# A decoder trunk on one Trainium2 core: side engines issued in source order through the Strassen groups of the feed-forward layers, with their first loads three steps sooner

## The chip, the cores and the metric

One core of one Trainium2 chip runs the whole program. The metric is the device time of one execution in microseconds (us). The profiled execution gives, beside its own time, a span: the time from its first to its last recorded instruction. TensorE (PE in the profile) does the matmuls, VectorE (DVE) and ScalarE (ACT) the elementwise work, GpSimd (POOL) a little arithmetic and the accumulating DMAs, and sync (SP) starts the plain weight loads.

## The reference

Two layers, float32, a sequence of 512 tokens of width 1024. What the change touches is the feed-forward block, of which each layer has two (four in all):

```python
def swiglu(h, w_gate, w_up, w_down):
    return (jax.nn.silu(h @ w_gate) * (h @ w_up)) @ w_down
...
    f = swiglu(rms_norm(h, ffn1_pre_g[l]), ffn1_w_gate[l], ffn1_w_up[l], ffn1_w_down[l])
    h = h + FFN_RESIDUAL_SCALE * rms_norm(f, ffn1_post_g[l])
```

The hidden width is 2816, that is 22 blocks of 128 columns. Between the two feed-forward blocks of a layer stands a token mixer (`mixer`), which the change leaves alone.

## The kernel before

**Arithmetic.** Every float32 product is made of three matmuls on rounded parts: a weight tile is cut into a high part `wh` (ScalarE, L104 or L117) and the rest `wl` (VectorE, L105 or L118), an activation into `xh` and `xl`, and `mm3` (L145) adds `wh*xh`, `wh*xl` and `wl*xh` in PSUM (L147, L148, L149).

**One feed-forward block.** `boundary` ends the stage before, normalises, transposes (`turned`, L275) and multiplies the first two blocks of 128 hidden columns directly (`outer`, tiles `pf`: gate, up, gate, up). The other 20 blocks are done in 10 groups of two by a Strassen-Winograd scheme (`seven`, L466): a group has seven half products instead of eight, each of 24 matmuls of 128x256. A half product takes a sum of weight quarters (`s1` to `s4`, `a11`, `a12`, `a22`) and a sum of activation quarters (`nt1`, `nt2`, `t3`, `t4`, built by `quarter_sums` and `form`, tiles `t`, `th`, `tl`). After the groups `ffn` hands the products `gs` to the next `boundary`, which multiplies them by `w_down` (tiles `py`).

**A group step by step.** `step(g, r)` runs at t = 7g + r. It loads quarters with sync (`raw`, L480), adds further quarters onto them in SBUF by accumulating DMAs that GpSimd starts (`add`, L483), cuts each sum (`split_of`), and multiplies: a12 at r = 1, a11 at 2, s1 at 3, s2 at 5, s3 at 7, a22 at 11, s4 at 13. Groups overlap, so that in the steady state each t has one half product, in the order a12, a11, s1, a22 of the group before, s2, s4 of the group before, s3. Between products ScalarE copies a partial sum out of PSUM (`taken`, L499, tiles `n`) and VectorE adds it to other accumulators (`added`, L504). A group owns four PSUM tiles (`f0` and `f1`, two each, gate and up); each product fills the first tile of the pair with 12 matmuls, then the second. PSUM has eight such tiles, and four are held by `pf` until the first silu (`gate`, L452) and multiplication (`up`, L457).

**What sets the order.** A scheduler orders each engine's instructions by its own estimate of when each can start; only inside `tc.manual_schedule` do the named engines keep source order (before, only VectorE in a part of the mixer). Buffers are limited: 7 for raw chunks, 5 for each of `wh` and `wl`.

Of the kernel before, what the change touches and what calls it, by code (L numbers as in the profile page):

```python
# [30 lines left out]
CB = 8  # L31
# [3 lines left out]
LANES = (slice(0, 64), slice(64, P))  # L35

# [22 lines left out]
def build(tc, ws, x, vecs, gains, wdf, lamv, fb, consts, out):  # L59
# [3 lines left out]
    with ExitStack() as ctx:  # L63
# [12 lines left out]
        def nm(s):  # L76
            cnt[0] += 1
            return f"{s}{cnt[0]}"
# [173 lines left out]
        def boundary(post, pre, first):  # L252
# [7 lines left out]
            hs = [[None, None] for _ in range(NQ)]  # L260
            stat = np_.tile([P, 16], F32, tag="stat", name=nm("stat"))
# [140 lines left out]
            forms, t2 = {}, [None, None]  # L402
# [18 lines left out]
            for j, k in enumerate(range(4)):  # L421
# [26 lines left out]
        gs = []  # L448
# [6 lines left out]
        def up(pu, x, scale=1.0):  # L455
            u = slot(F32, "g")
            V.scalar_tensor_tensor(out=u, in0=pu, scalar=scale, in1=x, op0=ALU.mult, op1=ALU.mult)  # L457
            gs.append(u)
# [7 lines left out]
        def seven(wg, wu, l, forms):  # L466
# [8 lines left out]
            base = len(order) // CB  # L475
# [30 lines left out]
            def step(g, r):  # L506
                d = ga[g]

                if r == -5:
                    raw(g, "X", 2)  # L510
                if r == -4:
                    add(g, "X", 3)
                    raw(g, "Z", 1)
                if r == -3:
                    raw(g, "Y", 0)
                if r == -1:
                    split_of(g, "a12", "Z")
# [10 lines left out]
                if r == 6:  # L528
                    raw(g, "W", 3)
# [4 lines left out]

                if r == 1:
                    d["f0"] = [ps("f0") for _ in range(2)]
                    product(g, "a12", [p[:, HALVES[0]] for p in d["f0"]], "b21", True)
# [14 lines left out]
                if r == 11:  # L552
                    product(g, "a22", [p[:, HALVES[0]] for p in d["f1"]], "t4", False)
                    d["x1"] = gate(d["f1"][0], -1.0)
                if r == 13:
                    product(g, "s4", [p[:, HALVES[1]] for p in d["f0"]], "b22", False)
                    added(g, *[[p[:, HALVES[1]] for p in d["f0"]]] * 2, "n2")
                    up(d["f0"][1], gate(d["f0"][0]))
                    up(d["f1"][1], d["x1"], -1.0)
# [12 lines left out]
        def ffn(l, n, entry):  # L572
            steps, pf = entry
            for f in range(2):
                up(pf[2 * f + 1], gate(pf[2 * f]))
# [7 lines left out]
            ys = gs[:]  # L583
            gs.clear()
            return 3 * l + 2 * n - 2, 0.5, f"ffn{n}_w_down", l, ys
# [464 lines left out]
```

## Time and profile before

| | before |
|---|---|
| time, median of 3 runs | 2723.58 us (2722.3 to 2725.3) |
| time of the profiled execution | 2721.85 us |
| its span | 2720.1 us |
| TensorE busy | 2659.3 us, 98% |
| VectorE, ScalarE, GpSimd busy | 61%, 44%, 9% |
| mean granted clock of TensorE | 0.994 |

The profiled execution is 1.73 us under the median; 1.75 us of its time lie outside its span. Matmuls are pipelined and a row's end is modelled, so consecutive rows overlap: what a matmul costs is read from the distance of starts, not from its own duration. "Idle before" is the time in which an engine did nothing before an instruction, with the instruction that released it.

### The profile page before, as it was taken

What the parts mean: (1) busy time and instruction counts of PE and PEld (TensorE: products, weight loads), DVE (VectorE), ACT (ScalarE), POOL (GpSimd) and SP (SyncE); (2) the same over time, 40 slices, a digit from 0 to 9 for tenths busy, and PEclk for the clock granted to TensorE, in tenths of its full rate; (3) what the DMA queues carried; (4) which work ended last, traced back from release to release, by engine and by line L of the source; (5) the groups of instructions that cost most, each with busy time, mean ns of one, the idle gap of its engine ahead of it and who ended that gap; (6) DMA issues with size and microseconds to landing.
All of it is one profiled execution on the core that took longest, in us unless ns stands there. A gap on an engine that the chain in (4) does not pass through costs nothing. (4 is left out here: it accounts for less than half of the span.)

```text
span 2720.1 us, 39646 instructions
## 1 busy us (share of the span) xinstructions
PE 2659.3 (98%) x15764; PEld 2363.5 (87%) x15764; DVE 1658.8 (61%) x2715; ACT 1204.7 (44%) x2031; POOL 233.9 (9%) x306
## 2 busy tenths in 40 slices
PE   6999999999999999999989999999999999999998
PEld 6999888888888888998889998888888888889987
DVE  5556358777785456565365563596786754555642
ACT  5545242355553335544255552424545533454541
POOL 2110000000000011110021100000010000211100
PEclk9999999999999999999999999999999999999999
DMA  7886433222222356885358863332222223578740
GB/s 202 201 209 181 133 117 101 86 78 86 90 86 90 96 176 147 206 201 170 114 136 206 205 198 102 118 97 81 71 89 97 82 90 102 162 177 207 196 154 33
DMA packets 110105, 365.26 MB, mean 134 GB/s; under 512 B 12496, under 2 KB 12880, under 8 KB 109920
## 3 DMA queue, kind: packets, MB, share of 16 engines
q1 hardware_dynamic: 68688, 246.45, 26.7%
q0 software_dynamic: 23040, 83.90, 17.5%
q10 hardware_dynamic: 18192, 32.40, 3.5%
q8 instruction: 123, 2.02, 0.3%
q14 instruction: 62, 0.51, 0.1%
HBM read 350.07 MB, written 12.62 MB: 133 GB/s over the span
## 5 line engine op out<-in xcount | busy, mean ns | idle before, releaser
L117 ACT CAST wh<-raw 128x1024 fp32r<-128x1024 f32 (+1 forms) x305 | 319.9, 1049 | 728.7 <-PE p L148 347.8
L118 DVE TENSOR_TENSOR wl<-raw,wh 128x1024 fp32r<-128x1024 f32 (+1 forms) x305 | 371.6, 1220 | 395.6 <-ACT wh L117 393.1
L105 DVE TENSOR_TENSOR wl<-raw,wh 128x1024 fp32r<-128x1024 f32 x280 | 342.5, 1223 | 315.4 <-ACT wh L104 314.9
L104 ACT CAST wh<-raw 128x1024 fp32r<-128x1024 f32 x280 | 293.8, 1049 | 313.2 <-PE f L148 210.5
L147 PE MATMUL p<-xh,wh 128*128 128x512 f32 x1024 | 404.3, 395 | 0.0
L149 PE MATMUL p<-xh,wl 128*128 128x512 f32 x1024 | 399.4, 390 | 0.0
L148 PE MATMUL p<-xl,wh 128*128 128x512 f32 x1024 | 398.8, 389 | 0.0
L147 PE MATMUL f<-th,wh 128*128 128x256 f32 x1280 | 369.5, 290 | 3.5 <-DVE f L504 3.5
L148 PE MATMUL f<-tl,wh 128*128 128x256 f32 x1280 | 364.0, 285 | 0.0
L149 PE MATMUL f<-th,wl 128*128 128x256 f32 x1280 | 358.6, 285 | 0.0
L147 PE MATMUL f<-xh,wh 128*128 128x256 f32 x960 | 273.9, 285 | 20.4 <-ACT s L452 20.4
L236 PE MATMUL py<-wh,gh 128*128 128x512 f32 x704 | 274.4, 390 | 0.0
L238 PE MATMUL py<-wh,gl 128*128 128x512 f32 x704 | 274.1, 389 | 0.0
L237 PE MATMUL py<-wl,gh 128*128 128x512 f32 x704 | 274.1, 389 | 0.0
L148 PE MATMUL f<-xl,wh 128*128 128x256 f32 x960 | 273.0, 284 | 0.0
L149 PE MATMUL f<-xh,wl 128*128 128x256 f32 x960 | 272.8, 284 | 0.0
L147 PEld LDWEIGHTS f<-th,wh 128*128 128x128 f32 x1280 | 248.1, 194 | 8.4 <-DVE f L504 6.0
L148 PEld LDWEIGHTS f<-tl,wh 128*128 128x128 f32 x1280 | 248.2, 194 | 0.0
L149 PEld LDWEIGHTS f<-th,wl 128*128 128x128 f32 x1280 | 245.4, 194 | 0.0
L483 POOL DMA_DIRECT2D raw<-ws x160 | 138.7, 867 | 1143.2 <-DMA raw<-ws 614.8
L149 PEld LDWEIGHTS p<-xh,wl 128*128 128x128 f32 x1024 | 192.3, 188 | 40.9
L148 PEld LDWEIGHTS p<-xl,wh 128*128 128x128 f32 x1024 | 192.6, 188 | 39.0 <-issue 0.5
(211 smaller groups left out, 4809.7 us busy)
## 6 DMA issues: line engine op xcount, KB each, us to landing
raw<-ws SPq DMA_DIRECT2D x463, 512.0 KB, 3.6
raw<-ws POOLq DMA_DIRECT2D x160, 512.0 KB, 5.6
hd<-h ACTq DMA_DIRECT2D x40, 256.0 KB, 2.1
h<-hd ACTq DMA_DIRECT2D x40, 256.0 KB, 5.3
cb<-cum ACTq DMA_DIRECT2D x16, 256.0 KB, 3.5
gb<-gains ACTq DMA_DIRECT2D x12, 256.0 KB, 4.3
h<-x SPq DMA_DIRECT2D x8, 256.0 KB, 4.8
h<-x ACTq DMA_DIRECT2D x8, 256.0 KB, 5.4
```

The costliest lines, as they stand in the source:

```text
L104: S.copy(out=wh, in_=raw)
L105: V.tensor_sub(out=wl, in0=raw, in1=wh.bitcast(F32))
L117: S.copy(out=wh[:, j], in_=raw[:, j])
L118: V.tensor_sub(out=wl[:, j], in0=raw[:, j], in1=wh[:, j].bitcast(F32))
L147: PE.matmul(out=out, lhsT=w[0], rhs=x[0], start=first, stop=False, skip_group_check=free)
L148: PE.matmul(out=out, lhsT=w[0], rhs=x[1], start=False, stop=False, skip_group_check=free)
L149: PE.matmul(out=out, lhsT=w[1], rhs=x[0], start=False, stop=last, skip_group_check=free)
L236: PE.matmul(out=out, lhsT=x[0][:, r], rhs=w[0], start=first, stop=False)
L237: PE.matmul(out=out, lhsT=x[0][:, r], rhs=w[1], start=False, stop=False)
L238: PE.matmul(out=out, lhsT=x[1][:, r], rhs=w[0], start=False, stop=last)
L483: G.dma_start(out=ga[g][key], in_=ws[base + 4 * g + u], accum_op=ALU.add)
```

## The change

The set `SIDE` (ScalarE, VectorE, GpSimd, sync) is put under `manual_schedule` from the start of a block's Strassen part to the end of its groups. TensorE stays with the scheduler. `step` is split in two: `fed` (loads, adds, cuts) runs for all groups of a t before `step` (products and what follows them). X, Z and Y are loaded three, three and two steps sooner (r = -8, -7, -5), W two steps sooner; the forms `t3` and `t4` are built inside the groups, at t = 2 and 7; the last multiplication of a group moves to r = 14, that of its second half to r = 12. The set of instructions of every engine stays the same.

```diff
+SIDE = {getattr(mybir.EngineType, n) for n in ("Activation", "DVE", "Pool", "SP")}
...
             if post is None:
+                ordered.enter_context(tc.manual_schedule(engines=SIDE))
                 turned(us[0:2], 0)
             whole()
+            base = len(order) // CB + PLAIN
...
+            if post is not None:
+                ordered.enter_context(tc.manual_schedule(engines=SIDE))
+            forms, t2, later = {}, [None, None], []
...
-            steps = seven(first[0][0][0], first[1][0][0], first[0][0][1], forms)
+            steps = seven(first[0][0][0], first[1][0][0], first[0][0][1], base, forms, later)
+            for _ in range(7):
+                next(steps)
             for k in range(KD - 2, KD):
                 outer(k, HALVES[0])
             for k in range(KD):
+                if k in (0, 3):
+                    next(steps)
                 outer(k, HALVES[1])
-                if k == 0:
-                    nt1 = quarter_sums(ALU.subtract, b11, b12)
-                    form("nt1", nt1)
-                if k == 2:
-                    t2 = quarter_sums(ALU.add, b22, nt1)
+                if k == 1:
+                    t2[:] = quarter_sums(ALU.subtract, b11, b12)
+                    form("nt1", t2)
+                if k == 4:
+                    t2[:] = quarter_sums(ALU.add, b22, t2)
                     form("nt2", t2, True)
-                if k == 4:
-                    form("t3", quarter_sums(ALU.subtract, b22, b12))
-                if k == 6:
-                    form("t4", quarter_sums(ALU.subtract, t2, b21))
-                if k < 6:
-                    next(steps)
-            return steps, pf
+            later.append(lambda: form("t3", quarter_sums(ALU.subtract, b22, b12)))
+            later.append(lambda: form("t4", quarter_sums(ALU.subtract, t2, b21)))
+            return (steps, ordered), pf
...
-            def step(g, r):
-                d = ga[g]
-
-                if r == -5:
+            def fed(g, r):
+
+                if r == -8:
                     raw(g, "X", 2)
-                if r == -4:
+                if r == -7:
                     add(g, "X", 3)
                     raw(g, "Z", 1)
-                if r == -3:
+                if r == -5:
                     raw(g, "Y", 0)
                 if r == -1:
-                    split_of(g, "a12", "Z")
                     split_of(g, "s1", "X")
                     add(g, "X", 0)
+                    split_of(g, "a12", "Z")
...
-            for t in range(-5, 7 * GROUPS + 7):
+            for t in range(-8, 7 * GROUPS + 8):
...
-                for g in range(GROUPS):
-                    if -5 <= t - 7 * g <= 13:
-                        step(g, t - 7 * g)
+                for do in fed, step:
+                    for g in range(GROUPS):
+                        if -8 <= t - 7 * g <= 14:
+                            do(g, t - 7 * g)
+                if t in (2, 7):
+                    later.pop(0)()
                 yield t
```

How the instructions move is shown at three places. The number in a name is a buffer's; the kernel's lines shift by one to six in the changed file (L147 is now L148, L452 is L458, L499 is L504).

First, ScalarE at the start of the second block's groups, before:

```order
L104 CAST wh1777_9713<-raw1744_9512 128x1024
L168 CAST th1747_9542<-t1745_9538 128x512
L104 CAST wh1781_9746<-raw1775_9709 128x1024
L168 CAST th1749_9546<-t1746_9539 128x512
L104 CAST wh1783_9750<-raw1772_9677 128x1024
L168 CAST th1759_9592<-t1757_9588 128x512
L168 CAST th1761_9596<-t1758_9589 128x512
L452 ACT_TABLE_LOAD
L452 ACTIVATE s1763_9612<-pf1719_9297 128x512
L452 ACTIVATE s1765_9616<-pf1721_9299 128x512
L499 COPY n11771_9672<-f11769_9646 128x256
L499 COPY n11771_9672<-f11770_9647 128x256
```

and with the change:

```order
L169 CAST th1742_9502<-t1739_9495 128x512
L105 CAST wh1744_9518<-raw1732_9433 128x1024
L171 ACTIVATE th1749_9554<-t1747_9550 128x512
L171 ACTIVATE th1751_9558<-t1748_9551 128x512
L458 ACT_TABLE_LOAD
L458 ACTIVATE s1753_9598<-pf1719_9300 128x512
L458 ACTIVATE s1755_9602<-pf1721_9302 128x512
L504 COPY n11762_9660<-f11760_9634 128x256
L504 COPY n11762_9660<-f11761_9635 128x256
L169 CAST th1765_9669<-t1763_9665 128x512
L169 CAST th1767_9673<-t1764_9666 128x512
L105 CAST wh1769_9677<-raw1730_9428 128x1024
```

The two silus stood behind all eight forms and the cuts of later products; now they stand behind four forms, and the forms of `t3` (`th1765`, `th1767`) and the cut of s2 (`wh1769`) follow the copies out of a11.

Second, TensorE at the same start, where a11 of the first group ends, before:

```order
L147 MATMUL f11770_9647<-xh1695_9219,wh1755_9571 128x256
L148 MATMUL f11770_9647<-xl1696_9220,wh1755_9571 128x256
L149 MATMUL f11770_9647<-xh1695_9219,wl1756_9572 128x256
L147 MATMUL f01788_9789<-xh1698_9228,wh1781_9746 128x256
L148 MATMUL f01788_9789<-xl1699_9229,wh1781_9746 128x256
L149 MATMUL f01788_9789<-xh1698_9228,wl1782_9747 128x256
```

and with the change:

```order
L148 MATMUL f11761_9635<-xh1695_9222,wh1744_9518 128x256
L149 MATMUL f11761_9635<-xl1696_9223,wh1744_9518 128x256
L150 MATMUL f11761_9635<-xh1695_9222,wl1745_9519 128x256
L148 MATMUL f01757_9606<-th1740_9498,wh1733_9459 128x256
L149 MATMUL f01757_9606<-tl1741_9499,wh1733_9459 128x256
L150 MATMUL f01757_9606<-th1740_9498,wl1734_9460 128x256
```

Behind a11 stood a12 of the second group (`f01788`, a PSUM tile that `pf` has to give up); now s1 of the first group follows, into the group's own `f01757`, then s2 and s3, and only then the second group.

Third, ScalarE at the end of the first block's groups, before (`wh402` is the cut of the last a22, `wh405` that of the first `w_down` chunk, `wh407` that of the last s4):

```order
L104 CAST wh402_2866<-raw400_2835 128x1024
L452 ACTIVATE s387_2758<-f1351_2435 128x512
L117 CAST wh405_2871<-raw404_2870 128x1024
L499 COPY n2390_2788<-f1380_2670 128x256
L168 CAST gh391_2791<-g120_585 128x512
L168 CAST gh393_2795<-g122_589 128x512
L104 CAST wh407_2876<-raw354_2466 128x1024
L499 COPY n2390_2788<-f1381_2671 128x256
```

and with the change (`n3401` is the copy that waits for the last s3):

```order
L458 ACTIVATE s399_2835<-f0349_2412 128x512
L504 COPY n3401_2863<-f1380_2672 128x256
L504 COPY n3401_2863<-f1381_2673 128x256
L105 CAST wh402_2868<-raw387_2736 128x1024
L118 CAST wh405_2873<-raw404_2872 128x1024
L105 CAST wh407_2878<-raw342_2343 128x1024
```

The three cuts stood ahead of the copies out of s3, that of a22 even ahead of the copies out of s2; now all three stand behind the copies out of s3.

## Rows read from the trace of the kernel before

**Rows 1.** The page: each engine's busy time, share of the span and instructions.

```profile
PE 2659.3 (98%) x15764; PEld 2363.5 (87%) x15764; DVE 1658.8 (61%) x2715; ACT 1204.7 (44%) x2031; POOL 233.9 (9%) x306
```

**Rows 2.** Waits of TensorE: engine line <- releaser: total us, times, longest.

```profile
PE f L147 <- ACT s L452: 20.4, 4, 6.5
...
PE f L147 <- DVE f L504: 3.5, 5, 1.3
```

**Rows 3.** TensorE's timeline, three of the silu waits (start, us, instruction [idle before]).

```profile
58.96 0.39 PE L147 MATMUL f<-xh,wh 128*128 128x256 f32 x1 [2.01 <-ACT s L452]
...
1044.46 0.58 PE L147 MATMUL f<-xh,wh 128*128 128x256 f32 x1 [6.49 <-ACT s L452]
...
1405.03 0.58 PE L147 MATMUL f<-xh,wh 128*128 128x256 f32 x1 [5.37 <-ACT s L452]
```

**Rows 4.** Windows behind the waits: us, busy by engine, PEclk (granted), DMA share, GB/s.

```profile
59.60:63.00 3.40, 3.40 (x18) 3.40 (x18) 2.53 (x5) 1.27 (x4) 0.86 (x1) 0.51 0.50 155
1044.50:1049.40 4.90, 4.90 (x23) 4.90 (x24) 1.90 (x4) 0.94 (x3) 0.00 (x0) 0.50 0.65 107
1049.50:1060.00 10.50, 10.50 (x89) 10.40 (x88) 4.76 (x6) 5.48 (x8) 1.73 (x2) 1.00 0.44 101
1405.10:1411.20 6.10, 5.45 (x24) 5.15 (x25) 2.94 (x6) 0.90 (x3) 0.86 (x1) 0.50 0.58 120
2391.90:2397.60 5.70, 5.70 (x27) 5.70 (x28) 1.92 (x4) 0.95 (x3) 0.00 (x0) 0.50 0.53 95
...
95.50:98.90 3.40, 2.10 (x18) 2.07 (x18) 2.80 (x4) 1.31 (x2) 0.63 (x1) 1.00 0.56 105
```

**Rows 5.** ScalarE's timeline at the start of the second block's groups.

```profile
1042.52 1.28 ACT L452 ACT_TABLE_LOAD   x1
1043.81 1.08 ACT L452 ACTIVATE s<-pf 128x512 f32<-128x512 f32 x2
```

**Rows 6.** TensorE's timeline there: the first matmul of the first group.

```profile
1032.06 0.28 PE L147 MATMUL f<-xh,wh 128*128 128x256 f32 x1
```

**Rows 7.** Groups by line and form, 100 to 250 us: busy, mean ns of one, idle before.

```profile
L104 ACT CAST wh<-raw 128x1024 fp32r<-128x1024 f32 x51 | 53.4, 1047 | 57.4 <-PE f L148 40.0 <-DMA raw<-ws 13.9 <-ACT n L499 1.6
L499 ACT COPY n<-f 128x256 f32<-128x256 f32 x44 | 16.2, 369 | 8.6 <-PE f L149 8.6
...
L105 DVE TENSOR_TENSOR wl<-raw,wh 128x1024 fp32r<-128x1024 f32 x51 | 62.4, 1223 | 59.7 <-ACT wh L104 59.4
L504 DVE TENSOR_TENSOR f<-f,n 128x256 f32<-128x256 f32 x42 | 18.0, 428 | 2.6 <-PE f L149 2.5
L457 DVE SCALAR_TENSOR_TENSOR g<-f,s 128x512 f32<-128x512 f32 x14 | 9.0, 686 | 0.7
```

**Rows 8.** Timelines of VectorE and ScalarE: forming one activation sum (t, th, tl).

```profile
1035.89 1.29 DVE L417 TENSOR_TENSOR t<-xf,xf 128x512 f32<-128x512 f32 x2
...
1039.96 0.68 DVE L161 TENSOR_TENSOR tl<-t,th 128x512 fp32r<-128x512 f32 x1
...
1036.88 0.61 ACT L168 CAST th<-t 128x512 fp32r<-128x512 f32 x1
```

**Rows 9.** Timelines of ScalarE and VectorE in the first block, before its groups.

```profile
18.90 1.05 ACT L104 CAST wh<-raw 128x1024 fp32r<-128x1024 f32 x1 [0.27 <-DMA raw<-ws]
...
25.91 0.84 ACT L170 ACTIVATE xh<-pt,vec 128x256 fp32r<-128x256 f32 x2 [0.58 <-DVE xl L163]
...
35.53 2.81 ACT L170 ACTIVATE xh<-pt,vec 128x256 fp32r<-128x256 f32 x7 [6.31 <-PE pt L284]
...
23.98 0.48 DVE L163 SCALAR_TENSOR_TENSOR xl<-pt,vec,xh 128x256 fp32r<-128x256 f32 x1
```

**Rows 10.** A window with the end of the first block's groups; waits for loads; landing of L483.

```profile
200.00:300.00 100.00, 100.00 (x674) 92.76 (x673) 60.00 (x78) 49.94 (x75) 6.04 (x7) 1.00 0.65 188
...
ACT wh L104 <- DMA raw<-ws: 72.1, 36, 3.3
...
DMA to landing us min/median/max: 5.1/5.6/9.0
```

More of the change, by code (lines that the diff above doesn't have):

```diff
@@ L260, in boundary @@
             hs = [[None, None] for _ in range(NQ)]
+            ordered = ExitStack()
             stat = np_.tile([P, 16], F32, tag="stat", name=nm("stat"))
@@ L400, in boundary @@
                 return xs, pf
-            forms, t2 = {}, [None, None]
+            if post is not None:
+                ordered.enter_context(tc.manual_schedule(engines=SIDE))
+            forms, t2, later = {}, [None, None], []
             def form(name, srcs, negate=False):
@@ L420, in boundary @@
             b11, b12, b21, b22 = ([xf[b + 2 * r][h] for b in range(2)] for r in range(2) for h in range(2))
-            for j, k in enumerate(range(4)):
+            for k in range(4):
                 forms.setdefault("b11", []).append(tuple(v[:, HALVES[0]] for v in xs[k]))
@@ L428, in boundary @@
             for k in range(KD):
+                if k in (0, 3):
+                    next(steps)
                 outer(k, HALVES[1])
-                if k == 0:
-                    nt1 = quarter_sums(ALU.subtract, b11, b12)
-                    form("nt1", nt1)
-                if k == 2:
-                    t2 = quarter_sums(ALU.add, b22, nt1)
-                    form("nt2", t2, True)
-                if k == 4:
-                    form("t3", quarter_sums(ALU.subtract, b22, b12))
-                if k == 6:
-                    form("t4", quarter_sums(ALU.subtract, t2, b21))
-                if k < 6:
-                    next(steps)
-            return steps, pf
+                if k == 1:
[3 more added lines that the diff above has]
+                    t2[:] = quarter_sums(ALU.add, b22, t2)
+                    form("nt2", t2, True)
+            later.append(lambda: form("t3", quarter_sums(ALU.subtract, b22, b12)))
+            later.append(lambda: form("t4", quarter_sums(ALU.subtract, t2, b21)))
+            return (steps, ordered), pf
         def ffn_first(l, n):
             return [[(f"ffn{n}_w_{w}", l, k, f * P) for k in range(KD)] for f in range(2) for w in ("gate", "up")]
-        gs = []
+        gs = {}
         def gate(pg, scale=1.0):
@@ L457, in up @@
             V.scalar_tensor_tensor(out=u, in0=pu, scalar=scale, in1=x, op0=ALU.mult, op1=ALU.mult)
-            gs.append(u)
+            return u
         def halves(src):
@@ L464, in halves, with seven @@
             return hi, lo
-        def seven(wg, wu, l, forms):
-            base = len(order) // CB
+        def seven(wg, wu, l, base, forms, later):
             ga = [{} for _ in range(GROUPS)]
@@ L527, in step @@
                     split_of(g, "s3", "Y")
-                if r == 6:
+                if r == 4:
                     raw(g, "W", 3)
@@ L533, in step @@
                     split_of(g, "s4", "X")
+            def step(g, r):
+                d = ga[g]
                 if r == 1:
@@ L554, in step @@
                     d["x1"] = gate(d["f1"][0], -1.0)
+                if r == 12:
+                    gs[2 * g + 3] = up(d["f1"][1], d["x1"], -1.0)
                 if r == 13:
@@ L557, in step @@
                     added(g, *[[p[:, HALVES[1]] for p in d["f0"]]] * 2, "n2")
-                    up(d["f0"][1], gate(d["f0"][0]))
-                    up(d["f1"][1], d["x1"], -1.0)
+                if r == 14:
+                    gs[2 * g + 2] = up(d["f0"][1], gate(d["f0"][0]))
                     d.clear()
-            for t in range(-5, 7 * GROUPS + 7):
+            for t in range(-8, 7 * GROUPS + 8):
                 if t == 1:
@@ L566, in seven @@
                             order.extend((w, l, r + k, (2 * g + 2 + c) * P) for w in (wg, wu) for k in range(4))
-                for g in range(GROUPS):
-                    if -5 <= t - 7 * g <= 13:
-                        step(g, t - 7 * g)
+                for do in fed, step:
[4 more added lines that the diff above has]
+                    later.pop(0)()
                 yield t
         def ffn(l, n, entry):
-            steps, pf = entry
+            (steps, ordered), pf = entry
             for f in range(2):
-                up(pf[2 * f + 1], gate(pf[2 * f]))
+                gs[f] = up(pf[2 * f + 1], gate(pf[2 * f]))
             for t in steps:
@@ L582, in ffn @@
                     load(c)
-            ys = gs[:]
+            ordered.close()
+            ys = [gs[f] for f in range(KF)]
             gs.clear()
```

## The prediction

> **What bounds the kernel now.** I read the page first: TensorE is busy 98% of the span, no other engine over 61% [rows 1]. So only what TensorE waits for can be won, and only what makes it wait can be lost. Its waits come next [rows 2]: 20.4 us in four waits of a matmul into `f` for the silu of L452, one in each feed-forward block, and 3.5 us in five waits for an addition of L504. The timeline gives them singly: 2.01, 6.49 and 5.37 us in the first three blocks [rows 3]; the fourth is the longest, 6.5 us. Then the windows [rows 4]: behind each of the four, for 3.4 to 6.1 us the granted clock is 0.50 or 0.51, the lower of its two levels (1.2 of 2.4 GHz). There 23 matmuls take 4.9 us, 0.213 us each; right after, at full clock, 89 take 10.5 us, 0.118 us each. A half product of 24 matmuls thus lasts 2.83 us. In the groups' steady state TensorE has nothing to win: the window that holds the last groups and the end of a block is 100% busy [rows 10].
>
> The cause of a silu wait is seen on ScalarE [rows 5]: the first group starts at 1032.06 [rows 6], its a12 and a11 are over 5.7 us later, and the next matmul in TensorE's order needs a PSUM tile that `pf` still holds. The silu that frees it stands behind all eight forms and starts at 1043.81, after a table load of 1.28 us.
>
> All sums below are against the profiled execution, 2721.85 us; the median of the runs is 1.73 us more.
>
> **What goes.** With the change the silus stand behind four forms, and TensorE goes on with s1, s2 and s3 of its own group before it needs a tile of `pf`. I count all 20.4 us as gone, and the 3.5 us too: in source order the copy and the addition of a11 come right when a11 ends, with no cut in between. The lower clock behind the old waits goes with them: 3.4, 4.9, 5.45 (busy of 6.1) and 5.7 us [rows 4] at 0.213 instead of 0.118 lose 45%, 8.7 us. In the first block a cut stood in front of the last normalised tile, on ScalarE at 18.90 [rows 9] and with its `wl` (1.22 us [rows 7]) on VectorE; it now comes after the transposes, so that the first `xl` moves up from 23.98 by about 1.1 us. I take 0.9, between 0 and 1.2. Gone: 20.4 + 3.5 + 8.7 + 0.9 = 33.5 us.
>
> **What comes: the start of the groups, blocks 2 to 4.** Now s2 follows s1 directly, with no product of another group between. Its cut stands on ScalarE behind the copies out of a11 and the two forms of t3; these need VectorE, which does the additions first. From the end of a11: second copy 0.37, second addition 0.43 [rows 7], two `t` 1.29, second `th` 0.61 [rows 8], cut 1.05: 3.75 us. s1 covers 2.83. TensorE waits 0.9, does the four matmuls that need `wh` alone (0.5) and waits 0.7 more for `wl` (1.22 behind the cut): 1.6 us. In the second group a cut of W stands before the additions that s1 waits for: 0.5, between 0 and 1.3, the longest that such a wait took [rows 2]. The cuts of a12 and a11 of the second group are covered by s3 and by matmuls on `wh` alone: nothing. If that cover were gone, it would cost one `wl`, 1.2 us.
>
> **The end of the groups, all blocks.** The last s3 is followed at once by the last a22, whose cut stood earlier in the order and now stands behind the copies that wait for s3. Second copy 0.37 and cut 1.05 [rows 7] make 1.4 us; four matmuls on `wh` alone follow; then two of `py`, whose own cut is next in ScalarE's order, about 0.5 us more. I take 1.9 us, between 0 (the scheduler fills it with `py`) and 2.6 (copy, cut and `wl` one after another).
>
> **The first block's start.** Here manual order begins before the transposes. ScalarE does two `xh` and two `xf` on one PSUM tile before it goes to the next, and a second `xh` waits for VectorE's `xl` (0.58 [rows 9]), where the scheduler had run seven `xh` in a row in 2.81 us. One tile takes four such steps of 0.48 and two of 0.37, four tiles 10.7 us: from 35.53 - 1.1 = 34.4 to 45.1. Then come, one after another, cut 1.05, two `wl` 2.4, two `t` 1.3, two `tl` 1.3, `wl` 1.2, two `t` 1.3, `th` 0.6, table load 1.28, two silus 1.08, `g` 0.69, addition 0.43 [rows 5, 7, 8]: 12.6 us, to 57.7. s1 is due earlier: the old wait began at 58.96 - 2.01 = 56.95, 48 matmuls before it the groups began at 51.3, now at 50.2, and a11 ends at 55.9. s1 waits 1.8 us, s2 then 1.2. The old wait of 2.01 us was followed by the lower clock; I charge this one the same 3.4 us x 45% = 1.5.
>
> **Queues that are moved past.** SP only holds loads, in the same order as before; GpSimd's additions wait for VectorE's cuts, and one that waits holds up the next. An accumulating load lands after 5.6 us, at most 9.0 [rows 10]. s2's cut comes three half products and a copy after its quarter is free, some 9 us: covered, narrowly at the maximum. The loads three steps sooner gain nothing by themselves: ScalarE waited 72.1 us for loads [rows 10], in a stretch where TensorE did not wait.
>
> **Sum.** Blocks 2 to 4: 3 x (1.6 + 0.5 + 1.9) = 12.0. Block 1: 1.8 + 1.2 + 0.5 + 1.9 + 1.5 = 6.9. Gone less come: 33.5 - 18.9 = 14.6 us. The other seven places wait 1.4 to 2 us each in two pieces; the window with the wait of 1.3 us for an addition (TensorE busy 2.10 of 3.40 us) keeps a clock of 1.00 [rows 4], a wait of 2.01 was followed by the lower one. The charge is 0 to 7 x 1.5; I take one, 1.5 us. That leaves 13.1: 2721.85 - 13.1 = 2708.8, or 2710.5 beside the median. I say 2710.
>
> The clock, against the notes: a wait of 2.01 us [rows 3] was followed by a clock of 0.51 [rows 4]. The Trainium skill ("TensorE: Matmul & The Clock Gate", HAM oscillation) lets the clock fall only after idle gaps longer than any wait forecast here; the trace disagrees at 2.01 us. By that rule no charge for the clock would stand, and the sum would give 2706.
>
> The PSUM tile, against the notes: s1 now follows a11 into the tile that VectorE still adds to, and TensorE has waited for such additions [rows 2]. The Trainium skill ("Perfetto Trace Analysis", Matmuls) wants matmul groups that follow each other to go to different PSUM banks, so that emptying one overlaps the next; that speaks against the new order. By it each block would lose a copy and an addition, 0.8 us, 3.2 in all; by the rows both end within the 1.4 us that the second half of a product takes, and in blocks 2 to 4 nothing is lost.
>
> **Rivals.** *All covered:* ScalarE and VectorE sit idle enough at the starts and ends that none of the new waits shows. For it: the scheduler kept matmuls on `wh` and two of `py` as fillers. Against it: the chains above are longer than one half product. Time: 2721.85 - 33.5 = 2688. *Given back:* the new waits are as forecast, but the lower clock follows nearly all of them (9 us more), or they stand at the upper ends (1.3 and 2.6, 6 us more): 2718 to 2726. For it: two waits close together make nearly 2 us. *Slower:* source order blocks ScalarE in the steady state. Behind s2 stand a copy, the cut of s1, the cut of a12 and its `wl`, 0.37 + 1.05 + 1.05 + 1.22 = 3.7 us, against two products, 5.7 us: 2.0 us to spare. The cut of s1 waits for an accumulating load. Before, such waits lasted 2.0 us in the mean (72.1 in 36) and at most 3.3 [rows 10], and nothing stood behind them. From 2.0 us on they fall on TensorE: at 3.3 it is 1.3 us in each of 36 groups, 47 us, so 2709 to 2756, say 2740. Against it: the first load of a group now starts three products sooner, 8.5 us. *Not what it says:* seven raw buffers may keep the loads from starting sooner; that gains and costs nothing as long as it stays under the 2.0 us, and is part of the forecast.
>
> **Chances.** Forecast 0.58 (its own range 2702 to 2717), all covered 0.12, given back 0.17, slower 0.13. A measurement here can tell about 0.2%, 5.4 us, from no change. Faster than that: 0.69; within it 0.18; slower 0.13. The range takes in the forecast, half of the covered case and most of the given back: 2698 to 2724.
>
> **What would show it.** Right: no wait of `f` for L458 over 1 us in blocks 2 to 4; waits of 0.7 to 0.9 us before s2 of the first group and about 1.4 us before the last a22; a wait of some 2 us for an addition (L509) in the first block; full windows in between. Wrong: waits of a matmul for `wh` or `wl` that repeat in every group (the slower case), the lower clock behind the new waits (given back), or a wait for the silu that stays.

## The result and the profile after

The changed kernel takes 2701.36 us (median of four runs, 2699.78 to 2704.5) against 2724.43 before (its median with a fourth run): a ratio of 0.9918, 95% interval 0.9901 to 0.9935. It is faster, inside the forecast range, 8.6 us under the forecast of 2710. A second set of four runs gave 2703.38 (2701.91 to 2704.75). The profiled execution took 2704.5 us, 17.35 less than that of before.

The page and TensorE's waits after, to be held against [rows 1] and [rows 2]:

```profile
PE 2654.9 (98%) x15764; PEld 2359.8 (87%) x15764; DVE 1652.2 (61%) x2715; ACT 1196.0 (44%) x2031; POOL 234.7 (9%) x306
```

```profile
...
PE f L148 <- ACT wh L105: 8.2, 7, 1.4
PE pf L149 <- DVE xl L164: 7.1, 6, 2.0
PE f L150 <- DVE wl L106: 2.9, 7, 0.5
PE f L148 <- DVE f L509: 2.5, 1, 2.5
PE py L237 <- ACT wh L118: 0.8, 4, 0.2
```

The wait for the silu, 20.4 us before, is gone from the list. In its place stand two kinds of short waits for a cut (`wh`, `wl`), seven each, and one for an addition. TensorE's timeline gives them one by one (the first block's; then two of s2 and one of the second group in block 2; then the two at that block's end):

```profile
59.01 0.39 PE L148 MATMUL f<-th,wh 128*128 128x256 f32 x1 [2.54 <-DVE f L509]
...
1042.19 0.39 PE L148 MATMUL f<-th,wh 128*128 128x256 f32 x1 [0.84 <-ACT wh L105]
1043.45 0.38 PE L150 MATMUL f<-th,wl 128*128 128x256 f32 x1 [0.52 <-DVE wl L106]
1055.78 0.38 PE L150 MATMUL f<-th,wl 128*128 128x256 f32 x1 [0.33 <-DVE wl L106]
...
1232.63 0.38 PE L148 MATMUL f<-th,wh 128*128 128x256 f32 x1 [1.41 <-ACT wh L105]
1233.58 0.72 PE L237 MATMUL py<-wh,gh 128*128 128x512 f32 x2 [0.21 <-ACT wh L118]
```

ScalarE's timeline at the start of block 2 shows why. The silu that started at 1043.81 [rows 5] now starts at 1034.60, behind four forms. What s2 needs now stands last on ScalarE: the copies out of a11, the two `th` of t3, then its cut at 1041.10.

```profile
1032.05 1.23 ACT L171 ACTIVATE th<-t 128x512 fp32r<-128x512 f32 x2 [1.89 <-DVE t L423]
1033.30 1.28 ACT L458 ACT_TABLE_LOAD   x1
1034.60 1.09 ACT L458 ACTIVATE s<-pf 128x512 f32<-128x512 f32 x2
1037.07 0.37 ACT L504 COPY n<-f 128x256 f32<-128x256 f32 x1 [1.38 <-PE f L150]
1038.51 0.37 ACT L504 COPY n<-f 128x256 f32<-128x256 f32 x1 [1.07 <-PE f L150]
1039.97 1.23 ACT L169 CAST th<-t 128x512 fp32r<-128x512 f32 x2 [1.09 <-DVE t L423]
1041.10 1.99 ACT L105 CAST wh<-raw 128x1024 fp32r<-128x1024 f32 x2
```

Windows of the kernel after (us, busy by engine, granted clock, DMA share, GB/s): behind the first block's wait; behind the waits at the end of block 1; on the two waits at the end of block 2, and behind them; the same pair for block 3; behind the waits at the end of block 4; on the waits of s2 in block 2.

```profile
60.10:63.50 3.40, 3.40 (x19) 3.40 (x18) 3.01 (x5) 2.98 (x4) 0.00 (x0) 0.51 0.31 60
254.70:258.10 3.40, 3.40 (x19) 3.40 (x18) 1.82 (x2) 1.48 (x3) 0.00 (x0) 0.50 0.77 217
1231.00:1234.30 3.30, 1.69 (x10) 1.20 (x10) 2.12 (x3) 3.04 (x4) 0.00 (x0) 1.00 0.00 0
1234.30:1237.70 3.40, 3.40 (x19) 3.40 (x18) 1.81 (x2) 1.52 (x3) 0.00 (x0) 0.50 0.75 202
1587.80:1591.20 3.40, 1.79 (x11) 1.43 (x11) 2.38 (x3) 3.21 (x4) 0.00 (x0) 1.00 0.00 0
1591.20:1594.60 3.40, 3.40 (x30) 3.40 (x30) 2.73 (x4) 1.53 (x2) 0.00 (x0) 1.00 0.82 264
2568.90:2572.30 3.40, 3.40 (x18) 3.30 (x17) 2.08 (x2) 1.30 (x3) 0.00 (x0) 0.50 0.74 192
1041.30:1044.70 3.40, 2.03 (x15) 1.78 (x15) 2.98 (x4) 1.79 (x2) 0.86 (x1) 1.00 0.01 2
```

The clock was at half (1.2 GHz) behind the first block's wait and the ends of blocks 1, 2 and 4, and not at the end of block 3, though the waits there are the same (1.41 and 0.21 us at all four).

The trace cut at the `pf` matmul that waits for `xl` at the start of each stage gives a length for every feed-forward block (the last ends with the last matmul); in brackets TensorE's idle time between the two cuts, and what it worked at half clock (us). Two experiments stand beside it, for later.

| block | before | after | forms later only | all three moves |
|---|---|---|---|---|
| 1 | 357.9 (4.4; 3.4) | 360.3 (5.5; 6.8) | 356.2 (4.2; 0) | 351.6 (1.1; 0) |
| 2 | 361.5 (8.7; 5.0) | 356.6 (4.8; 3.4) | 356.2 (5.2; 0) | 351.3 (1.6; 0) |
| 3 | 362.8 (9.3; 5.5) | 355.1 (4.9; 0) | 358.6 (5.9; 3.4) | 351.3 (1.6; 0) |
| 4 | 359.8 (8.3; 5.8) | 353.7 (3.8; 3.4) | 354.8 (4.3; 3.0) | 348.3 (0.6; 0) |

The length less the idle time less 45% of the half-clock time (what the matmuls lose at half clock, 0.213 us each for 0.118) lies between 347.8 and 352.0, and within one row the four differ by at most 1.6: idle time and clock explain the differences but for that. The mixers (623.0 us each) did not change. Block 1 became longer, blocks 2 to 4 shorter by 4.9, 7.7 and 6.1.

### The profile page after: what moved, and what is told of

Same layout as the page of the kernel before. It is cut to its first block, busy times and chain, and to the rows that moved or that the text cites. A ratio compares the mean times of both kernels' runs of the same rounds, so it can differ in the third digit from the quotient of the medians.

```text
span 2702.7 us, 39690 instructions
## 1 busy us (share of the span) xinstructions
PE 2654.9 (98%) x15764; PEld 2359.8 (87%) x15764; DVE 1652.2 (61%) x2715; ACT 1196.0 (44%) x2031; POOL 234.7 (9%) x306
## 3 DMA queue, kind: packets, MB, share of 16 engines
q8 instruction: 123, 2.02, 0.3%
## 4 chain that ended last, share of the span: by engine, by line
PE 89%; DVE 5%; ACT 3%; issue 1%; POOL 1%; DMA 0%; ACTq 0%; DVEq 0%; POOLq 0%
PE p L148 11%; PE p L149 10%; PE p L150 10%; PE f L150 9%; PE f L148 9%; PE f L149 9%; PE py L237 6%; PE py L239 6%; PE py L238 6%; PE o L773 1%; PE pv L238 1%; PE pv L237 1%; PE pv L239 1%; PE pt L757 1%; PE pf L149 1%
## 5 line engine op out<-in xcount | busy, mean ns | idle before, releaser
L106 DVE TENSOR_TENSOR wl<-raw,wh 128x1024 fp32r<-128x1024 f32 x280 | 335.5, 1222 | 200.9 <-ACT wh L105 200.9
L148 PE MATMUL p<-xh,wh 128*128 128x512 f32 x1024 | 404.1, 395 | 0.0
L148 PE MATMUL f<-th,wh 128*128 128x256 f32 x1280 | 365.2, 286 | 10.7 <-ACT wh L105 8.2
L105 ACT CAST wh<-raw 128x1024 fp32r<-128x1024 f32 x280 | 282.3, 1050 | 1.1 <-DMA raw<-ws 1.1
L148 PE MATMUL f<-xh,wh 128*128 128x256 f32 x960 | 271.7, 283 | 0.0
L148 PEld LDWEIGHTS f<-th,wh 128*128 128x128 f32 x1280 | 248.4, 194 | 12.6 <-ACT wh L105 9.6
L148 PEld LDWEIGHTS p<-xh,wh 128*128 128x128 f32 x1024 | 192.6, 188 | 38.7 <-PE pt L757 0.5
```

Source lines behind the costliest of these rows:

```text
L105: S.copy(out=wh, in_=raw)
L106: V.tensor_sub(out=wl, in0=raw, in1=wh.bitcast(F32))
L148: PE.matmul(out=out, lhsT=w[0], rhs=x[0], start=first, stop=False, skip_group_check=free)
```

## The experiments

All ratios are to the kernel before on the same chip, with 95% intervals. Differences under some 0.2% (5 us) are not told apart.

**The order with the old loads.** The loads of a group go back to their old steps.

```diff
-                if r == -8:
+                if r == -5:
                     raw(g, "X", 2)
-                if r == -7:
+                if r == -4:
                     add(g, "X", 3)
...
-                if r == -5:
+                if r == -3:
                     raw(g, "Y", 0)
...
-                if r == 4:
+                if r == 6:
                     raw(g, "W", 3)
```

> The source order of the change is kept, but the loads of a group are begun at their old steps (X at -5 and -4, Y at -3, W at 6). My theory: the gain comes from the order at the start of a block, not from the loads. Then TensorE still has no wait for a silu, the starts and ends of the blocks wait as in the changed kernel, and the time is that of the changed kernel, 2701 us within 0.2% (2696 to 2706), unless the order has to have the earlier loads. Rival, the loads are needed: in source order the cut of s1 waits for its accumulating load with a copy, another cut and a wl behind it and 2.0 us to spare; begun three half products (8.5 us) later, the load comes too late in every group and TensorE waits up to 1.3 us in each of 36 groups: 2715 to 2750 us, with waits of f for wh or wl that repeat in the steady state.

Measured: 2870.22 us, ratio 1.0525 (1.051 to 1.054). My theory fell; the rival's mechanism is there, at more than three times its price. TensorE's waits in this run:

```profile
PE f L148 <- ACT wh L105: 78.5, 43, 6.8
PE f L150 <- DVE wl L106: 31.2, 35, 1.0
```

One of its groups in the timeline, first on TensorE, then on ScalarE:

```profile
122.53 0.39 PE L148 MATMUL f<-xh,wh 128*128 128x256 f32 x1 [1.03 <-ACT wh L105]
123.98 0.58 PE L150 MATMUL f<-xh,wl 128*128 128x256 f32 x1 [0.94 <-DVE wl L106]
...
120.49 2.94 ACT L105 CAST wh<-raw 128x1024 fp32r<-128x1024 f32 x3 [4.33 <-DMA raw<-ws]
```

ScalarE's cuts on the page (busy, mean ns | idle before), and a window of 100 us as above:

```profile
L105 ACT CAST wh<-raw 128x1024 fp32r<-128x1024 f32 x280 | 282.6, 1048 | 180.5 <-DMA raw<-ws 180.5
```

```profile
100.00:200.00 100.00, 90.94 (x696) 89.30 (x697) 50.45 (x67) 41.91 (x64) 14.94 (x17) 0.93 0.75 176
```

TensorE is busy 90.94% of these 100 us at a mean clock of 0.93; the kernel after is at 100% and 1.00 there.
The first of three cuts in a row is that of s1, which waits 4.33 us for its load; the cut of a12 stands behind it, and a12 (`xh`) is what TensorE waits for. The Trainium skill ("PSUM — Partial Sum Buffer", Engine vs sequencer instructions) says that ScalarE's queue is strictly first in, first out; the trace agrees, with 4.33 us in front of the cut of a12, which then ran without a wait for its own load. Against the changed kernel TensorE idles 98.6 us more and works 124.5 us more at half clock (45% are 56): 155 of the 165.5 us between the spans. In the kernel after, the same row of the page has 1.1 us of waiting where this one has 180.5:

```profile
L105 ACT CAST wh<-raw 128x1024 fp32r<-128x1024 f32 x280 | 282.3, 1050 | 1.1 <-DMA raw<-ws 1.1
```

**How much sooner they must be.** All loads one step later than in the change:

```diff
-                if r == -8:
+                if r == -7:
                     raw(g, "X", 2)
...
-                if r == 4:
+                if r == 5:
                     raw(g, "W", 3)
```

> The changed kernel with the loads of X, Y and W one step (2.83 us) later, so two steps sooner than before instead of three. With the old steps the source order took 2870 us: in nearly every group s2 or s1 waited for a cut that waited for its load. In the changed kernel no cut of L105 shows among ScalarE's main waits for a load. Theory: the time to spare for the cut of s1 is about 2 us, as the prediction had it (3.7 us behind it against two products of 5.7), and a load that is 2.8 us later eats most of it: no wait to 0.8 us in each of 36 groups, 2701 to 2730, say 2705. Rival, the margin is gone already with three steps less, so waits grow by 2.8 us less than in the run with old steps, where they were about 2 us: none, 2701 us. Rival, the accumulating loads queue behind each other on GpSimd, so that one step matters as much as three: over 2740 us.

Measured: 2704.63 us, ratio 0.9925 (0.991 to 0.994); the waits of the `f` matmuls are those of the kernel after, to 0.1 us. The time is the 2705 of my theory, but by chance: the wait that was to make it is not there, and the run stands for the rival without new waits. Then Y and W at their steps of before, X and Z one step sooner than before:

```diff
-                if r == -8:
+                if r == -6:
                     raw(g, "X", 2)
-                if r == -7:
+                if r == -5:
                     add(g, "X", 3)
                     raw(g, "Z", 1)
```

> The changed kernel with Y and W at their old steps and X and Z one step (2.83 us) sooner than before, where the changed kernel has three. With everything at the old steps a12 of the next group waited 0.7 to 2.5 us for its cut, which stands on ScalarE behind the cut of s1, and then 0.95 for its wl: 2870 us. Theory: X, whose first load has an accumulating load behind it, is what was late, and by less than one step; with one step more no wait repeats in the groups: 2701 to 2706 us. Rival, Y or W are late too, or the accumulating loads take longer the closer they follow each other: waits of up to 1 us stay in each group, with the lower clock behind some of them: 2715 to 2790 us.

Measured: 2702.14 us, ratio 0.9913 (0.9896 to 0.993). My theory holds. So of the earlier loads one step of X (and Z with it; the two were not tried apart) counts; its other steps, and Y's and W's, do nothing that can be told here. It is a cliff: one step of 2.83 us decides about 168 us, since without it nearly every group has its wait and mostly a fall of the clock.

**The loads and forms without the order.** The lines that enter `manual_schedule` are taken out.

```diff
-                ordered.enter_context(tc.manual_schedule(engines=SIDE))
...
-            if post is not None:
-                ordered.enter_context(tc.manual_schedule(engines=SIDE))
```

> The source of the change (forms of t3 and t4 later, loads sooner, the second silu of a group later), but the scheduler decides the order on all engines as before. Its order puts the first silu behind four forms and three cuts instead of eight forms and four cuts, and TensorE goes from a11 over to the second group's a12 instead of s1, s2 and s3 of its own. My theory: the forms that are gone from in front of the silu (four at 0.61 us on ScalarE and as many on VectorE) take 2 to 5 us from each of the four waits of 5.1 us in the mean; the rest of the gain needs the order. Then a silu wait of 1 to 3 us is left in blocks 2 to 4, and the time is 2705 to 2716 us. Rival, the later forms alone give everything and the source order nothing: 2695 to 2703 us, no silu wait. Rival, the source order gives everything: 2718 to 2726 us, silu waits of about 6 us stay.

Measured: 2706.10 us, ratio 0.9929 (0.9916 to 0.9943): no silu wait, most of the gain. The time lies in my theory's range, but the silu wait of 1 to 3 us that was to make it is not there; the later forms took it away without the order. One wait is new. The cut of s1, now ahead of that of a12 in the source, stands before the first `xh`, and its load is not there (timelines of ScalarE and TensorE):

```profile
26.72 1.04 ACT L105 CAST wh<-raw 128x1024 fp32r<-128x1024 f32 x1 [6.73 <-DMA raw<-ws]
27.67 0.47 ACT L171 ACTIVATE xh<-pt,vec 128x256 fp32r<-128x256 f32 x1
...
28.19 1.22 PE L148 MATMUL pf<-xh,wh 128*128 128x256 f32 x4 [7.65 <-ACT xh L171]
```

**The forms alone.** The kernel before, with `t3` and `t4` made inside the groups and nothing else.

```diff
-                if k == 4:
-                    form("t3", quarter_sums(ALU.subtract, b22, b12))
-                if k == 6:
-                    form("t4", quarter_sums(ALU.subtract, t2, b21))
...
+            later.append(lambda: form("t3", quarter_sums(ALU.subtract, b22, b12)))
+            later.append(lambda: form("t4", quarter_sums(ALU.subtract, t2, b21)))
...
+                if t in (2, 7):
+                    later.pop(0)()
```

> The kernel before with one part of the change alone: the forms t3 and t4 are made at steps 2 and 7 of the groups instead of before them. No source order, the loads at their old steps, the second silu where it was. The run without source order left TensorE no wait for a silu and took 2706.1 us, of which 7.65 us went into a wait at the very start (before 2.12 us) for a cut that stood there in front of the first xh; that cut is not there in this kernel. My theory now: the later forms are what removes the silu waits, and by themselves they give what the whole change gives: 2706.1 less 5.5 is 2700.6 us, between 2697 and 2704, same as the changed kernel's 2701.4. Rival, the loads three steps sooner are part of it: without them the scheduler's order waits for loads, 2707 to 2720 us. Rival, my theory before the runs, the source order is part of it: 2705 to 2716 us with silu waits of 1 to 3 us.

Measured: 2707.45 us (2705.76 to 2709.24), ratio 0.9934 (0.9921 to 0.9946): 17 of the 20 to 23 us. No wait for a silu is left, as I had it; the size I missed, because I took 7.65 less 2.12 us of the run above as its loss. It had put 7.65 us in the place of 1.17 + 2.04 here, and saved 1.8 us of other waits in block 1, so that only 2.1 us are left: 380.5 us to the end of block 1 here, 382.6 there. Blocks 3 and 4 here took them back, with 4.5 us more: TensorE worked 3.4 and 3.0 us at half clock (2.9 us lost), where the profiled execution of the run above has no fall in a block. What is left here are waits for cuts at the start of blocks 2 and 4, for additions in the course of the groups, and longer ones of the transposes at three boundaries. The time also lies in the range of the rival with the loads, but no such wait is seen: the cut behind the silu starts without one (below), and the same two waits for a cut stand in the run above, which has the earlier loads (2.28 and 2.02 us there, 2.01 and 2.03 here). TensorE's waits, and the timelines of ScalarE at the silu and of TensorE at one of the transposes:

```profile
PE f L147 <- DVE f L502: 5.6, 7, 1.5
PE f L147 <- ACT wh L104: 4.0, 2, 2.0
```

```profile
1035.87 1.28 ACT L450 ACT_TABLE_LOAD   x1
1037.16 0.60 ACT L450 ACTIVATE s<-pf 128x512 f32<-128x512 f32 x1
1037.66 1.04 ACT L104 CAST wh<-raw 128x1024 fp32r<-128x1024 f32 x1
...
1017.48 1.74 PE L284 MATMUL pt<-cst,u 128*128 128x128 f32 x12 [1.45 <-DVE u L272]
```

The profiled executions of this kernel and of the changed one are only 1.3 us apart (spans 2704.0 and 2702.7), the medians 4 to 6, about what can be told. So these runs do not show that source order and earlier loads add to the later forms.

**The order without the later forms.** `t3` and `t4` are made in front of the silus again.

```diff
-            later.append(lambda: form("t3", quarter_sums(ALU.subtract, b22, b12)))
-            later.append(lambda: form("t4", quarter_sums(ALU.subtract, t2, b21)))
+            form("t3", quarter_sums(ALU.subtract, b22, b12))
+            form("t4", quarter_sums(ALU.subtract, t2, b21))
```

> The source order of the change is kept, but the forms t3 and t4 are made in front of the silus again, so that the silus stand behind all eight forms; TensorE's order (s1, s2, s3 of its own group after a11) stays. My theory: that the silu comes late is the cause whichever matmul needs it first; the copies out of a11 stand behind the silus on ScalarE, so the wait comes back as a wait of s1 for the addition of a11: 4 to 8 us in each block with a lower clock behind it, less the 1.4 us that the waits before s2 take now: 2715 to 2730 us. Rival, TensorE's order alone covers the late silu (its own group has 8.5 us of matmuls before a tile of pf is needed): no wait over 1.5 us, 2696 to 2704 us.

Measured: 2714.31 us, ratio 0.9963 (0.995 to 0.9975). The silu starts at 1044.94, as late as before; the wait is there, under another name, as s1's for an addition: 7.8, 3.6, 2.4 and 3.6 us in the four blocks, smaller than I expected in blocks 2 to 4. The timelines of ScalarE and TensorE in block 2:

```profile
1042.46 1.17 ACT L169 CAST th<-t 128x512 fp32r<-128x512 f32 x2 [1.42 <-DVE t L423]
1043.65 1.28 ACT L458 ACT_TABLE_LOAD   x1
1044.94 1.08 ACT L458 ACTIVATE s<-pf 128x512 f32<-128x512 f32 x2
1045.91 0.66 ACT L504 COPY n<-f 128x256 f32<-128x256 f32 x2
...
1047.25 0.38 PE L148 MATMUL f<-th,wh 128*128 128x256 f32 x1 [3.61 <-DVE f L509]
```

So with late silus TensorE's own order covers a part of the wait in blocks 2 to 4: 9.6 us there, where the silu waits took 18.4 before. In block 1, where the source order begins before the transposes, 2.0 us became 7.8, and the ends of the blocks wait as in the changed kernel. The run as a whole, with its earlier loads, gains 10 us, an earlier silu alone 17. The two overlap; together they give 20 to 23.

**GpSimd left to the scheduler.** `SIDE` holds ScalarE and VectorE only.

```diff
-SIDE = {getattr(mybir.EngineType, n) for n in ("Activation", "DVE", "Pool", "SP")}
+SIDE = {getattr(mybir.EngineType, n) for n in ("Activation", "DVE")}
```

> The changed kernel with the source order held on ScalarE and VectorE alone; GpSimd's order is the scheduler's again, in which an accumulating load stands one to two loads later in its queue, and SyncE's is the same either way. Theory: loads in time are what lets ScalarE's source order run without a wait, and GpSimd's queue is where the accumulating loads wait for VectorE's cuts (608 us of its waits); a load that stands behind another load's cut comes some 3 to 6 us later and the cuts of s1 or s2 wait for it: 2705 to 2760 us. Rival, GpSimd's order is without effect, as the loads have time to spare: 2699 to 2704 us.

Measured: 2702.27 us (one run of four at 2708.93, unexplained), ratio 0.9927 (0.991 to 0.9944). The rival holds: ScalarE's cuts wait 21.6 us for loads instead of 1.1, and all but 0.7 us of it is covered.

**The ends of the blocks.** In the last group of a block W (its line is left out below) and its cut come two steps sooner, the cut of s4 three.

```diff
-                if r == 9:
+                if r == (9 if g < GROUPS - 1 else 7):
                     split_of(g, "a22", "W")
-                if r == 11:
+                if r == (11 if g < GROUPS - 1 else 8):
                     split_of(g, "s4", "X")
```

> Only in the last group of a block: W is loaded two steps sooner, its cut for a22 stands two steps earlier (in front of the copies that wait for s3), that of s4 three steps earlier. The changed kernel's trace has four waits of 1.41 + 0.21 us there (6.5 us), and behind three of them 3.41 us at half clock (1.5 us each). My theory: the waits and the clock falls behind them go, 4 x 1.62 + 3 x 1.5 = 11.0 us, so 2690 us against 2701 (between 2688 and 2696; the clock does not fall at the same three places in each execution). Rival, the wait moves: the cuts that now stand first make the copies of s3 late, and s4 or py waits for them as long: 2699 to 2704 us, same.

Measured: 2690.63 us (2689.25 to 2690.78), ratio 0.9871 (0.9858 to 0.9885), 10.7 us under the changed kernel. The waits of 1.41 and 0.21 us are gone from all four ends, and with them the falls of the clock there; of the seven waits for a cut `wh` the three of s2 are left:

```profile
PE f L148 <- ACT wh L105: 2.5, 3, 0.8
```

**The starts of blocks 2 to 4.**

```diff
-                if t in (2, 7):
+                if t in (3, 7):
                     later.pop(0)()
```

> The changed kernel with the forms of t3 one step later (step 3 instead of 2), so behind the cut of s2 in source order. In the changed kernel s2 of the first group waits 0.84 + 0.52 us in blocks 2 to 4 and 0.32 in block 1. Theory: the cut of s2 stands 3.75 us after a11's end because of the two additions, two t and a th in front of it; without the t and th, s2 does not wait, 4.4 us gone, and s3, which needs t3, waits 0.5 to 0.9 us in its place: net 1 to 3 us, 2698 to 2701. Rival, the wait only moves to s3 at its full size: 2701 us or more.

Measured: 2696.81 us (2692.22 to 2698.49), ratio 0.9892 (0.9879 to 0.9906). The waits of s2 went and none came before s3: better than expected, 5.1 us by the waits (1.36 + 0.33 in three blocks; the 0.33 of block 1 stays), 4.6 by the medians. The four ends and one wait for `wl` are left:

```profile
PE f L148 <- ACT wh L105: 5.6, 4, 1.4
...
PE f L150 <- DVE wl L106: 0.3, 1, 0.3
```

**The first block.** `manual_schedule` is entered behind the transposes in all blocks, and a12's cut comes first in group 0.

```diff
             if post is None:
-                ordered.enter_context(tc.manual_schedule(engines=SIDE))
                 turned(us[0:2], 0)
...
-            if post is not None:
-                ordered.enter_context(tc.manual_schedule(engines=SIDE))
+            ordered.enter_context(tc.manual_schedule(engines=SIDE))
...
+                    if g == 0:
+                        split_of(g, "a12", "Z")
                     split_of(g, "s1", "X")
```

> The changed kernel with the source order in the first block entered behind the transposes, as in the other blocks, so that the scheduler orders ScalarE's copies out of the transposes; and for the first group of a block the cut for a12 stands in front of that for s1 (else the cut that waits for the accumulating load would stand in front of the first xh, as in the run without source order, 5.7 us). Theory: the copies take 2.8 us in a row instead of 10.7 in steps, and the wait of s1 of 2.54 us goes with the 6.8 to 10 us at half clock behind it (45% of 6.8 is 3.1): 2.5 + 3.1 less about 1.3 for s2 waiting as in the other blocks, 4.3 us less: 2697 us, between 2694 and 2700. Rival, that chain of table load, silus and additions is the limit, not the copies, or the first start gets later again: 2700 to 2705.

Measured: 2699.21 us, ratio 0.9903 (0.9889 to 0.9916). The wait of 2.54 us is gone; s2 waits 0.90 + 0.52 us in its place, as expected. Block 1 lasts 355.7 us instead of 360.3, but the start before it 24.1 instead of 23.3. Of the 4.6 us, 1.5 are a fall of the clock at the end of block 1 that this execution did not have, which is not the edit's doing; behind the old wait the changed kernel had 3.4 us at half clock in both profiled executions, not the 6.8 that I charged. Of 4.3 us expected the medians show 2 to 4. The first silu of block 1, in the changed kernel and here:

```profile
56.70 1.08 ACT L458 ACTIVATE s<-pf 128x512 f32<-128x512 f32 x2
```

```profile
51.62 1.09 ACT L456 ACTIVATE s<-pf 128x512 f32<-128x512 f32 x2
```

**All three.**

> All three put together: the last group's cuts earlier (alone it gave 2690.6 us, 10.8 less than the changed kernel), the forms of t3 one step later, the source order of the first block behind the transposes. If they add up: 2690.6 less 1 to 3 less 4.3, 2684 to 2686 us. If the heads only move their wait: 2686 to 2688. If the first block gains nothing: 2688 to 2691.

Measured: 2682.71 us (2681.53 to 2683.55), ratio 0.9841 (0.9828 to 0.9854): 41.6 us faster than before, 18.7 to 20.7 faster than the change. This beats both kernels. The three moves alone gave 10.7, 4.6 and 2.2 against the first median: they add up within what can be told (17.5 for 18.7 to 20.7), a little better than the 2684 to 2686 expected. The edit is the three together. No `f` matmul waits any more; the whole list of TensorE's waits:

```profile
PE pt L286 <- DVE u L274: 19.2, 5, 15.8
PE pf L149 <- DVE xl L164: 7.5, 6, 2.4
PE pf L148 <- ACT xh L171: 0.8, 1, 0.8
PE pt L758 <- DVE e L826: 0.3, 2, 0.2
```

**The changed kernel once more.**

> The changed kernel once more, for the spread of its time and for the falls of the clock. Its first profiled execution had three falls to half clock of 3.41 us behind the waits of 1.41 + 0.21 us at the ends of the blocks and was the slowest of four (2699.8 to 2704.5). If the falls set the spread, an execution with n of them takes 2699.9 + 1.5 n us within 1 us; if they have nothing to do with it, the time varies by 5 us at the same number.

Measured: 2703.38 us (2701.91 to 2704.75). Its profiled execution had the same four falls as the first, at the same places, and took 2704.75; three of them lie at ends of blocks, so the rule gives 2704.4. It fits, but one number of falls tests little. The run with the forms of t3 one step later says more: its profiled execution had the same four waits of 1.41 + 0.21 us and no fall behind any; it took 2692.22 us, the other three 4.2 to 6.3 us more, which is 2.8 to 4.2 falls of 1.5 us. Those three have no trace; their mean granted clock is 0.997 where that of the first is 0.998, which fits, but four falls more would be 0.0025, so this stays an inference.

## Why the prediction was right

*What went.* All 20.4 us of silu waits went, and the lower clock behind them. The prediction gave two causes in one sentence, the forms moved behind the silus and TensorE's own s1 to s3; the runs take them apart in part: the first alone gave 17 us; the second, with the earlier loads and the source order, 10. The five waits for an addition went too; the one there is now is the new one of the first block. The first start moved up by 1.2 us (0.9 forecast, 0 to 1.2).

*What came, in blocks 2 to 4.* s2: 0.84 + 0.52 where the forecast had 0.9 + 0.7; the second group: 0.33 for 0.5; the ends: 1.41 + 0.21 for 1.4 + 0.5. Together 3 x 3.31 = 9.9 us for 12.0. The chains were right link by link; what was too large are mostly the second waits of each pair.

*Block 1.* s1 waited 2.54 us (1.8 forecast), s2 not at all (1.2), the second group 0.32, the end 1.62; with one fall of the clock (1.5) 6.0 us for 6.9. The run of the first block bears out ScalarE's stepwise copies as the cause: with the scheduler's order of them, and one cut less in front, the silu starts at 51.62 instead of 56.70 and the wait is gone; of these 5.1 us the copies make 4.3 (their last ends at 41.83 instead of 46.12).

*The clock.* One fall at the other seven places was charged, three came: 4.6 us for 1.5. None followed the 0.84 + 0.52 us of s2. The mis-sized step is that one; it went against the rest. The Trainium skill ("TensorE: Matmul & The Clock Gate", HAM oscillation) has the clock fall only after idle gaps longer than any of these waits; the trace disagrees, with 1.41 + 0.21 us of waiting and a granted clock of 0.50 behind it.

*Not in the sum.* The waits of the transposes at three boundaries fell from 1.15 to 1.31 us to 0.5 each (2.1), and the matmuls between the waits took 1.7 us less in all. Terms together against 13.1: 0.3 more at the start, 2.1 and 0.9 less of new waits, 2.1, 1.7, and 3.1 back for the clock: 17.1, against 17.35 measured between the profiled executions. That two gains which no step of the prediction had (2.1 and 1.7) outweigh the clock that it undercharged is luck. The rest of the distance to 2701.4 is that the profiled execution was the slowest of its four, while the forecast had added 1.7 us to the sum for the median.

*The PSUM tile.* The Trainium skill ("Perfetto Trace Analysis", Matmuls) wants matmul groups that follow each other in different banks. That speaks less against the new order than the prediction had it: a11 goes into `f1` and s1 into `f0`, so they do follow each other in different tiles; what s1 shares is the tile to which VectorE adds the copy of a11. In blocks 2 to 4 no wait of s1 for an addition is seen, so the rows were right there; in block 1 the wait is one for an addition, but it stands behind a late silu, as in the run with the forms first.

*The slower rival.* Its mechanism is real and was fenced off by the earlier loads, as the prediction said. Its price was not: 47 us at most in the prediction, about 168 with the old steps. The waits for `wh` alone came to 70 us more than in the changed kernel (78.5 for 8.2), as some took up to 6.8 us where 1.3 was the most forecast; the waits for `wl` behind them to 28 more, the lower clock to 56. "The loads three steps sooner gain nothing by themselves" is not contradicted, but no run shows them alone: with the scheduler's order the time went from 2707.5 to 2706.1, between runs that also differ in the place of the cuts and the second silu. The 72.1 us of waits for loads that the prediction puts in one stretch are the sum over the whole execution. With the source order an earlier load is the condition.

## What to carry to other kernels

Source order on a side engine makes each late transfer a wait of everything behind it, so give it only together with loads that are early enough, and find out by one step less where the cliff is. Ask first what stands in front of the late instruction and can be made later: here that alone gave about three quarters of the gain. With the fixed order nearly the same few waits stood in each block, and these could be read off and moved one at a time, for 19 to 21 us more; whether the same moves would do it under the scheduler's order was not tried.

## What the hardware did that was not expected

Waits of 1.41 and 0.21 us, 0.7 us apart, were followed by 3.41 us at half clock at the ends of blocks 1, 2 and 4 and not at that of block 3, at the same places in two profiled executions of the changed kernel and in those of the two runs with the loads one step later and nearly at their old steps. The same waits were followed by no fall at any end with the forms of t3 one step later and with GpSimd left to the scheduler, by one only, at the end of block 4, in the run of the first block, and by two, at blocks 1 and 3, in the run with the forms first. So equal waits of one program can cost 1.6 or 3.2 us. In the run with the old loads a pair of 1.03 and 0.94 us was followed by a fall too.
